# A fixed TensorE order and attention in five pieces, in a decoder layer of short convolution and retention

## The chip, the cores and the metric

The kernel runs on one core of one Trainium2 chip. The metric is the device time of one execution in microseconds; the time of a kernel is the median of its runs. Five engines matter: TensorE (PE in the profile; PEld is its weight load), VectorE (DVE), ScalarE (ACT), GpSimd (POOL) and SyncE (SP), which issues all the DMAs here. Each engine works through its own list of instructions in the order in which the list stands, and waits on semaphores for the others.

## The reference

One layer on 2048 rows of 1024 features with 16 learned meta rows ahead of them. The projection has eight parts of 512 columns: four for a gated convolution of width 3, four (q, k, v and a gate) for retention with four heads of 128. Retention is computed in chunks of 128 rows, with a state that is carried from chunk to chunk:

```python
hn = rms_norm(h, norm_g)
cx, cb, cc, cg, q, k, v, rg = jnp.split(hn @ w_in, N_PROJ, axis=-1)
conv_out = short_conv_branch(cx, cb, cc, conv_w) * silu(cg)
qf, kf = rotary(q) * RET_HEAD_DIM ** -0.5, rotary(k)
# per head and chunk of 128 rows
scores = (qc @ kc.T) * decay
inner = scores @ vc
upd = (kc * zeta).T @ vc
state = chunk_decay * state + upd            # cross uses the state before this chunk
cross = (qc * xi) @ state
ret = head_group_norm(inner + cross) * silu(rg)
out = rms_norm(h + concatenate([conv_out, ret]) @ w_out, final_g)
```

## The kernel before

Each float32 operand of a big product is split into a high and a low part (`wh`/`wl` for weights, `mh`/`ml` for the moving side), and three matmuls of 128x128 by 128x512 make one step; four steps, 12 matmuls, make one *product*. A *quad* computes a 2x2 block of results with seven such products (a Strassen-Winograd scheme, `quad`, matmul at L212). A *plain quad* (`quad_plain`, matmul at L262) does it with eight and needs no block sums; the first group, the first head of the second half and the first pair of output rows begin with plain quads. TensorE is fed from two rings of four PSUM banks: `pj` for the big products, `ms` for everything else.

The rows are handled in two halves (r = 0, 1). In each half the kernel goes through eight units: four convolution groups and four retention heads, in the order 4, 0, 1, 2, 3, 5, 6, 7 for r = 0 (4 is the first convolution group) and 0 to 7 for r = 1. Each unit has two quads: for a head first k and v, then q and the gate. After the second quad the head's attention follows in the source: for each half block j transposes of k and v (L631, L636), the state updates (L646), then for each j the scores (L659), the values (L669, L670), the norm on VectorE and GpSimd (L675 to L686), a transpose back (L693) and the gate with ret_norm_g (L694). The tile framework's scheduler decides at build time where each instruction stands on its engine; in before it mixes the pieces of a head's attention into the next unit's quads, and also orders single matmuls of the plain quads by when it expects their operands.

The start matters for the change. `moving` loads sixteen x tiles, scales them by norm1_g and splits them (L104, L105), with the first weight blocks in between (`begin`). After the eighth tile `normalise_meta` (L373 to L388) squares the meta tokens (L376), sums them on TensorE (L380), takes the root on VectorE and GpSimd (L275, L278), spreads it over the partitions (L285, L292, L295) and makes `meta_s` (L387, L388). `meta_products` (L390) multiplies `meta_s` with a unit's four raw weight blocks in 16 small matmuls (L397, two records each in the trace); its results feed the first state of each head and the first carry of each convolution group. For the first unit it is called, in the source, after `moving` and ahead of the first plain quad. While all this runs, `block_sums` (L174) and the splits of the second weights are queued on VectorE too.

Of the kernel before, what the change touches and what calls it, by code (L numbers as in the profile page):

```python
# [12 lines left out]
ALU = mybir.AluOpType  # L13

P = 128
D = 1024
SEQ = 2048
NMETA = 16
# [4 lines left out]
NR = 2  # L23
# [9 lines left out]
FIRST_W, PLAIN_W, B12 = 2, 3, 4  # L33
SUMS = (3, 2, 4, 6)

UNITS = (4, 0, 1, 2, 3, 5, 6, 7), (0, 1, 2, 3, 4, 5, 6, 7)
# [34 lines left out]
def hybrid_trunk(ctx: ExitStack, tc: tile.TileContext, t, out: bass.AP, chunk_decay):  # L71
# [14 lines left out]
    def ps_proj():  # L86
        return ps.tile([P, HB], F32, name="pj", tag="pj", bufs=4)

    def ps_misc():
# [113 lines left out]
    def quad(w, m, take):  # L203


        def product(i, bank, first):
            (wh, wl) = w[i]
            for kt in range(KH):
                ks = slice(kt * P, (kt + 1) * P)
                mh, ml = m[i][kt]  # L210
                for n, (a, b) in enumerate(((wl, mh), (wh, ml), (wh, mh))):
                    nc.tensor.matmul(  # L212
                        bank, a[:, ks], b, start=first and kt == 0 and n == 0, stop=kt == KH - 1 and n == 2,
                        skip_group_check=not first,
                    )

        def copy(bank):
            c = sb.tile([P, HB], F32, name="tc", tag="tc", bufs=COPIES)
            nc.scalar.copy(out=c, in_=bank)  # L219
            return c  # L220

        xb = ps_proj()
        product(0, xb, True)
        c = copy(xb)
        yb = ps_proj()
        product(1, yb, True)
        take(0, 0, yb, c)
        product(2, xb, False)
        u2 = copy(xb)
        zb = ps_proj()  # L230
        product(3, zb, True)
        c = copy(zb)
        product(4, xb, False)
        take(1, 1, xb, c)
        product(5, zb, False)
        take(0, 1, zb, u2)
        product(6, xb, False)
        take(1, 0, xb, None)

    def plain_part(n, load, slot):  # L240
# [10 lines left out]
    def quad_plain(w, m, take, middle=None):  # L251

        for j in range(2):
            banks = [ps_proj() for _ in range(2)]
            for half in range(2):
                for kt in range(KH):
                    ks = slice(kt * P, (kt + 1) * P)
                    mh, ml = m[BLOCK[half][j]][kt]
                    for i in range(2):
                        wh, wl = w[2 * i + half]  # L260
                        for n, (a, b) in enumerate(((wl, mh), (wh, ml), (wh, mh))):
                            nc.tensor.matmul(  # L262
                                banks[i], a[:, ks], b, start=half + kt + n == 0,
                                stop=half == 1 and kt == KH - 1 and n == 2,
                            )
            for i in range(2):
                take(i, j, banks[i], None)
            if middle and j == 0:
                middle()
# [120 lines left out]
    def meta_products(blocks, early=False):  # L390

        bank = ps_misc()
        four = [bank[i * 32 : i * 32 + NMETA, :P] for i in range(4)]
        with tc.high_priority(offset=HIGH) if early else nullcontext():
            for kt in range(KH):
                for i in (3, 2, 1, 0):
                    nc.tensor.matmul(  # L397
                        four[i], meta_s[:, i % 2 * KH + kt, :], blocks[i][:, kt * P : (kt + 1) * P],
                        start=kt == 0, stop=kt == KH - 1,
                    )  # L400
# [11 lines left out]
    def meta_state(h, scratch):  # L412
# [9 lines left out]
        add(nc.vector, k, a, b)  # L422
        up = ps_misc()
        nc.tensor.matmul(up[:, :P], k, v, start=True, stop=True)
        nc.scalar.copy(out=state[h], in_=up[:, :P])

    def meta_carry(g, scratch):

        cc, cx, u, _ = meta_sums(scratch)
        nc.vector.tensor_tensor(out=u, in0=cc, in1=cx, op=ALU.mult)  # L430
        tp = ps_misc()
        nc.tensor.transpose(tp[:, :NMETA], u, ident[:NMETA, :NMETA])
        nc.vector.tensor_copy(out=conv_carry[g], in_=tp[:, NMETA - 2 : NMETA])

# [29 lines left out]
    def group_plain(g, m, f, meta, first, between, ahead):  # L464
# [16 lines left out]
        quad_plain(first[0], m, take)  # L481
        meta_carry(g, meta)

# [31 lines left out]
    def conv_group(g, r, m, f, blocks, ahead):  # L515
# [20 lines left out]

        blocks, meta = blocks
        quad(stationary(blocks), m, take)
        if meta:
            meta_carry(g, meta)  # L540
        carry(u, g, r)
# [33 lines left out]
    def head(h, r, m, rot_t, f, blocks, ahead, first=(), between=()):  # L575


        between = iter(between)
        k, v = [None, None], [None, None]
        tables = [rot_t[:, :, j * HB : (j + 1) * HB] for j in range(2)]  # L580
# [17 lines left out]
        next(between, lambda: None)()  # L598
        q, sg = [None, None], [None, None]

# [21 lines left out]
        next(between, lambda: None)()  # L622
        if blocks[1]:
            meta_state(h, blocks[1])
        blocks = ahead()
        states = [state[h]]
        vt = []
        for j in range(2):
            tp = ps_misc()
            for c in range(CH):  # L630
                nc.tensor.transpose(tp[:, c * P : (c + 1) * P], k[j][:, c * P : (c + 1) * P], ident)  # L631
            kd = brief("kd")
            nc.scalar.mul(kd, tp, kd_col[:, h : h + 1])
            tp = ps_misc()
            for c in range(CH):
                nc.tensor.transpose(tp[:, c * P : (c + 1) * P], v[j][:, c * P : (c + 1) * P], ident)  # L636
            vj = v[j]
            for c in range(CH):
                cs = slice(c * P, (c + 1) * P)
                nc.scalar.mul(vj[:, cs], tp[:, cs], f[2][j][0][:, c : c + 1])  # L640
            vt.append(vj)
            last = r == NR - 1 and j == 1
            up = ps_misc()
            for c in range(CH - last):
                cs = slice(c * P, (c + 1) * P)
                nc.tensor.matmul(up[:, cs], kd[:, cs], vj[:, cs], start=True, stop=True)  # L646
            for c in range(CH - last):
                nxt = sb.tile([P, P], F32, name="state", tag="state", bufs=2 * CH)
                nc.vector.scalar_tensor_tensor(
                    out=nxt, in0=states[-1], scalar=chunk_decay[h], in1=up[:, c * P : (c + 1) * P],  # L650
                    op0=ALU.mult, op1=ALU.add,
                )
                states.append(nxt)

        for j in range(2):
            sc = ps_misc()
            for c in range(CH):
                cs = slice(c * P, (c + 1) * P)
                nc.tensor.matmul(sc[:, cs], k[j][:, cs], q[j][:, cs], start=True, stop=True)  # L659
            pm = brief("pm")  # L660
            nc.vector.scalar_tensor_tensor(
                out=pm.rearrange("p (c i) -> p c i", c=CH), in0=sc.rearrange("p (c i) -> p c i", c=CH),
                scalar=past_col[:, h : h + 1],
                in1=causal.rearrange("p (c i) -> p c i", c=1).broadcast_to([P, CH, P]), op0=ALU.mult, op1=ALU.mult,
            )
            o = ps_misc()
            for c in range(CH):
                cs = slice(c * P, (c + 1) * P)
                nc.tensor.matmul(o[:, cs], pm[:, cs], vt[j][:, cs], start=True, stop=False)  # L669
                nc.tensor.matmul(o[:, cs], q[j][:, cs], states[j * CH + c], start=False, stop=True)  # L670

            st = small.tile([P, CH, 6], F32, name="st", tag="st")
            mv = small.tile([P, CH, 2], F32, name="mv", tag="mv")
            for c in range(CH):
                nc.vector.bn_stats(out=st[:, c, :], in_=o[:, c * P : (c + 1) * P])  # L675
            for c in range(CH):
# [5 lines left out]
            nc.gpsimd.tensor_tensor(out=rp, in0=rs, in1=neg_half.rearrange("p (c a) -> p c a", a=1), op=ALU.pow)  # L682
            y = pm
            for c in range(CH):
                cs = slice(c * P, (c + 1) * P)
                nc.vector.tensor_scalar(  # L686
                    out=y[:, cs], in0=o[:, cs], scalar1=mv[:, c, 0:1], scalar2=rp[:, c, :],
                    op0=ALU.subtract, op1=ALU.mult,
                )
            yT = ps_misc()  # L690
            for c in range(CH):
                cs = slice(c * P, (c + 1) * P)
                nc.tensor.transpose(yT[:, cs], y[:, cs], ident)  # L693
            nc.vector.scalar_tensor_tensor(  # L694
                out=sg[j], in0=yT, scalar=ret_g[:, h : h + 1], in1=sg[j], op0=ALU.mult, op1=ALU.mult
            )
            store_mixed(r, j, KH + h, sg[j])
        if r < NR - 1:
            nc.gpsimd.tensor_copy(out=state[h], in_=states[-1])
        return blocks  # L700

# [202 lines left out]
```

## Time and profile before

| what | value |
|---|---|
| time, median of 3 runs | 895.5 us (894.32 to 895.67) |
| the profiled execution's own time | 893.76 us |
| its span, first to last instruction | 892.0 us |
| mean granted TensorE clock | 0.999 |
| matmuls at L212 and L262 | 3024 and 384 |

Rows of the timeline and of the chain begin with the start and the duration in us, then engine, line, operation, `out<-in`, shape and count; in brackets stands how long the engine was idle before and what ended that. Rows of the windows view begin with the stretch and its length; then come the busy time and the count of PE, PEld, DVE, ACT and POOL in it (fewer engines where the view was asked for one line, tile or engine), the granted clock, the DMA share and GB/s. Durations of neighbouring instructions overlap a little, so the spacing of starts is what one costs.

### The profile page before, as it was taken

To read this page: it belongs to the slowest core of one execution; us is meant where nothing else is said; L and a number is where in the kernel's file an instruction comes from. 1 tells how busy PE (TensorE), PEld (TensorE's weight loads), DVE (VectorE), ACT (ScalarE), POOL (GpSimd) and SP (SyncE) were. 2 spreads that over 40 slices of the span, in tenths; PEclk is the share of its full clock that TensorE was granted. 3 is DMA by queue.
4 is the path that set the end of the run, shared out by engine and by line. 5 is a ranking of instruction groups with operands and counts; after the bars stand their busy time and mean duration, and the time that the engine had idled before them with its cause. 6 is when DMAs were issued, how large, how long until landed. Compare 5 with 4: busy or idle time off the path is not lost.

```text
span 892.0 us, 12867 instructions
## 1 busy us (share of the span) xinstructions
PE 879.8 (99%) x4407; PEld 725.0 (81%) x4407; DVE 717.7 (80%) x1176; ACT 407.2 (46%) x816; POOL 397.8 (45%) x291
## 2 busy tenths in 40 slices
PE   8999999999999999999999999999999999999996
PEld 5778788888888778888888888888888888788885
DVE  6788887988967966999889899777668699766764
ACT  8674424234245364746243332423333476545553
POOL 0554222313134654452323323345546454787773
PEclk9999999999999999999999999999999999999999
DMA  9711224354224252834135272313131393555532
GB/s 336 231 65 48 72 54 150 129 159 149 73 83 142 83 154 75 293 117 141 48 95 200 71 245 87 96 58 95 49 93 49 117 390 101 183 165 160 183 121 81
DMA packets 76242, 116.94 MB, mean 131 GB/s; under 512 B 7632, under 2 KB 24336, under 8 KB 76176
## 3 DMA queue, kind: packets, MB, share of 16 engines
q1 hardware_dynamic: 76176, 116.11, 40.3%
q8 instruction: 35, 0.57, 0.3%
q14 instruction: 31, 0.25, 0.1%
HBM read 90.92 MB, written 25.17 MB: 130 GB/s over the span
## 4 chain that ended last, share of the span: by engine, by line
PE 82%; DVE 8%; DMA 4%; issue 2%; ACT 2%; POOL 2%; SPq 0%; POOLq 0%; DVEq 0%; ACTq 0%
PE pj L212 66%; PE pj L262 6%; DVE ml L113 2%; PE ms L669 1%; PE ms L670 1%; PE ms L659 1%; PE ms L646 1%; DMA w<-in_w_out 1%; DMA ra<-in_w_in 1%; PE ms L397 1%; DVE wl L113 1%; PE ms L693 1%; DVE ml L105 1%; PE ms L631 1%; PE ms L636 1%
## 5 line engine op out<-in xcount | busy, mean ns | idle before, releaser
L212 PE MATMUL pj<-mh,wl 128*128 128x512 f32 x1008 | 399.1, 396 | 1.5 <-ACT wh L101 0.6
L212 PE MATMUL pj<-ml,wh 128*128 128x512 f32 x1008 | 393.3, 390 | 0.0
L212 PE MATMUL pj<-mh,wh 128*128 128x512 f32 x1008 | 393.0, 390 | 0.0
L101 ACT CAST wh<-ra 128x512 fp32r<-128x512 f32 x216 | 134.0, 621 | 311.0 <-PE pj L212 264.9
L212 PEld LDWEIGHTS pj<-mh,wl 128*128 128x128 f32 x1008 | 189.4, 188 | 43.2 <-issue 2.2
L113 DVE TENSOR_TENSOR wl<-ra,wh 128x512 fp32r<-128x512 f32 x216 | 194.1, 899 | 34.5 <-ACT wh L101 34.0
L212 PEld LDWEIGHTS pj<-mh,wh 128*128 128x128 f32 x1008 | 189.2, 188 | 39.9
L212 PEld LDWEIGHTS pj<-ml,wh 128*128 128x128 f32 x1008 | 189.5, 188 | 37.8 <-issue 0.5
L113 POOL TENSOR_TENSOR ra<-ra 128x512 f32<-128x512 f32 x72 | 112.8, 1566 | 84.1 <-DVE qg L614 32.3
L110 POOL TENSOR_TENSOR sa<-ra 128x512 f32<-128x512 f32 x36 | 54.9, 1526 | 120.6 <-DVE wl L113 53.1
L113 POOL TENSOR_TENSOR ra<-sa,ra 128x512 f32<-128x512 f32 x36 | 52.0, 1444 | 92.6 <-DVE wl L113 89.1
L219 ACT COPY tc<-pj 128x512 f32<-128x512 f32 x108 | 62.7, 580 | 0.0
L262 PE MATMUL pj<-ml,mh 128*128 128x512 f32 x128 | 50.2, 392 | 0.1
L262 PE MATMUL pj<-mh,mh 128*128 128x512 f32 x128 | 49.9, 392 | 0.0
L262 PE MATMUL pj<-mh,ml 128*128 128x512 f32 x128 | 48.7, 397 | 0.7 <-DVE ml L113 0.6
L682 POOL TENSOR_TENSOR rp<-rs,neg_half 128x4 f32<-128x4 f32 x16 | 19.9, 1246 | 48.1 <-DVE rs L110 47.8
L723 DVE TENSOR_TENSOR yo<-pj,yo 128x512 f32<-128x512 f32 x32 | 21.9, 686 | 17.6 <-PE pj L212 7.8
L101 ACT CAST wh<-sa 128x512 fp32r<-128x512 f32 x36 | 22.4, 621 | 29.1 <-PE pj L212 28.9
L522 POOL TENSOR_TENSOR c<-c,rr 128x512 f32<-128x512 f32 x14 | 26.1, 1865 | 19.6 <-DVE c L459 9.6
L686 DVE TENSOR_SCALAR pm<-ms,mv,rp 128x128 f32<-128x128 f32 x64 | 21.9, 404 | 15.8 <-POOL rp L682 15.8
L522 POOL TENSOR_TENSOR c<-c,tc 128x512 f32<-128x512 f32 x14 | 26.1, 1862 | 18.7 <-ACT tc L548 18.7
L728 POOL TENSOR_TENSOR z<-yo,final_g 128x512 f32<-128x512 f32 x16 | 26.9, 1682 | 15.9 <-DVE yo L723 15.9
(137 smaller groups left out, 1145.5 us busy)
## 6 DMA issues: line engine op xcount, KB each, us to landing
ra<-in_w_in SPq DMA_DIRECT2D x128, 256.0 KB, 2.7
x<-in_xT SPq DMA_DIRECT2D x48, 256.0 KB, 4.8
w<-in_w_out SPq DMA_DIRECT2D x32, 256.0 KB, 5.2
ra<-mixed SPq DMA_DIRECT2D x32, 256.0 KB, 2.6
yo<-in_x SPq DMA_DIRECT2D x32, 256.0 KB, 4.5
ra<-in_x SPq DMA_DIRECT2D x16, 256.0 KB, 3.2
mixed<-c SPq DMA_DIRECT2D x16, 256.0 KB, 2.6
mixed<-qg SPq DMA_DIRECT2D x16, 256.0 KB, 2.3
```

Of the source, the lines that this page charges most:

```text
L101: nc.scalar.copy(out=hi, in_=src)
L105: nc.vector.scalar_tensor_tensor(out=lo, in0=src, scalar=scale, in1=hi.bitcast(F32), op0=ALU.mult, op1=ALU.subtract)
L110: eng.tensor_tensor(out=out, in0=a, in1=b, op=ALU.add)
L113: eng.tensor_tensor(out=out, in0=a, in1=b, op=ALU.subtract)
L212: nc.tensor.matmul(bank, a[:, ks], b, start=first and kt == 0 and n == 0, stop=kt == KH - 1 and n == 2, skip_group_check=not first,)
L219: nc.scalar.copy(out=c, in_=bank)
L262: nc.tensor.matmul(banks[i], a[:, ks], b, start=half + kt + n == 0, stop=half == 1 and kt == KH - 1 and n == 2,)
L522: eng.tensor_tensor(out=out, in0=a, in1=b, op=ALU.mult)
L682: nc.gpsimd.tensor_tensor(out=rp, in0=rs, in1=neg_half.rearrange("p (c a) -> p c a", a=1), op=ALU.pow)
L686: nc.vector.tensor_scalar(out=y[:, cs], in0=o[:, cs], scalar1=mv[:, c, 0:1], scalar2=rp[:, c, :], op0=ALU.subtract, op1=ALU.mult,)
L723: last[0] = nc.vector.tensor_tensor(out=y, in0=pp, in1=y, op=ALU.add)
L728: nc.gpsimd.tensor_tensor(out=ys[i][j], in0=y, in1=final_g[:, j * HB : (j + 1) * HB], op=ALU.mult)
```

## The change

Two things are changed. First, every big matmul, every attention matmul and transpose, and the meta products (all but the ones marked early) go through `pinned`, which ties each to the one before it in the source: the scheduler can no longer reorder these on TensorE. The warm-up, the small matmuls in `normalise_meta` and those in `spread` stay free.

Second, the attention of a head becomes five pieces. They are handed out at the head's start and called behind products that the table PLACES gives as (quads from here, product): for a head that is not the first (1, 1), (1, 6), (2, 1), (2, 4), (3, 1). So the first piece (transposes of block 0) comes in the head's second quad behind product 1; the second (transposes of block 1, meta state, updates of block 0) behind its last product; the third (updates of block 1, both scores) in the next unit's first quad behind product 1; the fourth (both values, with the norm) behind product 4; the last (both gates) in the next unit's second quad behind product 1, where the next head's first piece also stands. The meta state and the meta carry put their TensorE part into a function that is called at such a place.

```diff
+PLACES = ((1, 3), (1, 6), (2, 2), (2, 4), (3, 1)), ((1, 1), (1, 6), (2, 1), (2, 4), (3, 1))
...
+    def pinned(ins):
+        if last_pe:
+            tc.add_manual_dep(
+                ins.ins, last_pe.pop(),
+                mybir.DependencyInfo(mybir.DependencyClass.NoSync, mybir.DependencyReason.DATA), reason="order",
+            )
+        last_pe.append(ins.ins.name)
+    def matmul(*a, **k):
+        pinned(nc.tensor.matmul(*a, **k))
+    def transpose(*a):
+        pinned(nc.tensor.transpose(*a))
+    def at(quads, p, piece):
+        due.setdefault((count[0] + quads, p), []).append(piece)
+    def after_product(p):
+        for piece in due.pop((count[0], p), ()):
+            piece()
+        if p == 6:
+            count[0] += 1
...
         product(1, yb, True)
         take(0, 0, yb, c)
+        after_product(1)
...
+                if half == 0:
+                    after_product(3 * j)
+                    after_product(3 * j + 1)
             for i in range(2):
                 take(i, j, banks[i], None)
+            for p in (5, 6) if j else (2,):
+                after_product(p)
...
+        mm = nc.tensor.matmul if early else matmul
         with tc.high_priority(offset=HIGH) if early else nullcontext():
             for kt in range(KH):
                 for i in (3, 2, 1, 0):
-                    nc.tensor.matmul(
+                    mm(
...
+        for place, piece in zip(PLACES[h > 0], attention(h, r, f, k, v, q, sg, blocks[1])):
+            at(*place, piece)
...
+        def first():
+            if meta:
+                finish[0] = meta_state(h, meta)
+            turn(0)
+        def second():
+            turn(1)
+            finish[0]()
+            update(0)
+        def third():
+            update(1)
+            scores(0)
+            scores(1)
+        def fourth():
+            values(0)
+            values(1)
+            if r < NR - 1:
+                nc.gpsimd.tensor_copy(out=state[h], in_=states[-1])
+        def last():
+            gate(0)
+            gate(1)
+        return first, second, third, fourth, last
```

Three places in the order, row by row. The first is TensorE at the start, behind the warm-up. Before, the first rows and, in the second fence, the place of the first meta products further on (`meta_s`; `ra` are raw weight blocks, `pj` the products' banks, mh/ml the split operands):

```order
L262 MATMUL pj<-mh_115,ml_122 128x512
L262 MATMUL pj<-ml_116,mh_121 128x512
L262 MATMUL pj<-mh_115,mh_121 128x512
L262 MATMUL pj<-mh_115,ml_128 128x512
L262 MATMUL pj<-ml_116,mh_127 128x512
L262 MATMUL pj<-mh_115,mh_127 128x512
```

```order
L262 MATMUL pj<-mh_145,ml_281 128x512
L262 MATMUL pj<-ml_146,mh_280 128x512
L397 MATMUL ms<-ra,meta_s 16x128 x16
L262 MATMUL pj<-mh_145,mh_280 128x512
L262 MATMUL pj<-mh_145,ml_287 128x512
```

Now, right behind the warm-up (L423 are the sums of normalise_meta, L335 its spread, L104 every pinned matmul):

```order
L423 MATMUL ms<-ones,state_83 16x1 x8
L335 MATMUL ms<-rot,ones 128x16
L104 MATMUL ms<-ra,meta_s 16x128 x16
L104 MATMUL pj<-mh_115,ml_122 128x512
L104 MATMUL pj<-ml_116,mh_121 128x512
L104 MATMUL pj<-mh_115,mh_121 128x512
```

The meta products have moved from behind the 116th product to the head of the list, and the sums and the spread that they need stand ahead of them.

The second place is VectorE at the start, between the last splits of x and `meta_s` (`state_82` holds the meta tokens, `rm` their factors, `t` and `x` block sums). Before, the rows that end with it:

```order
L113 TENSOR_TENSOR ml_293<-ra,mh_292 128x512
L113 TENSOR_TENSOR ml_299<-ra,mh_298 128x512
L174 SCALAR_TENSOR_TENSOR x<-x,gain 128x512
L113 TENSOR_TENSOR ml_316<-x,mh_315 128x512
L174 SCALAR_TENSOR_TENSOR x<-x,gain 128x512
L387 TENSOR_TENSOR state_82<-state_82,rm 128x128
L113 TENSOR_TENSOR ml_320<-x,mh_319 128x512
L388 TENSOR_TENSOR meta_s<-state_82,gain 128x128
```

Now, from the last split of x on; ahead of these rows stand, behind the second t step (t_307), rs_v, five splits of x, the diagonal `rot` and three more splits:

```order
L136 SCALAR_TENSOR_TENSOR ml_253<-x,gain,mh_252 128x512
L144 TENSOR_TENSOR ml_281<-ra,mh_280 128x512
L205 SCALAR_TENSOR_TENSOR x<-x,gain,t_306 128x512
L144 TENSOR_TENSOR ml_287<-ra,mh_286 128x512
L430 TENSOR_TENSOR state_82<-state_82,rm 128x128
L205 SCALAR_TENSOR_TENSOR x<-x,gain,t_307 128x512
L144 TENSOR_TENSOR ml_293<-ra,mh_292 128x512
L144 TENSOR_TENSOR ml_299<-ra,mh_298 128x512
L205 SCALAR_TENSOR_TENSOR x<-x,gain 128x512
L431 TENSOR_TENSOR meta_s<-state_82,gain 128x128
```

`meta_s` has moved ahead by three rows of 512 columns and by an eviction of the first product that stood further up; the rest of the queue ahead of it is the same.

The third place is VectorE between a head's values and its gates (`st`, `mv`, `rs`, `rp`: the norm's statistics; `pm` its result; `kv` and `rot`: the next unit's k). Before, for block 0 of the first head; block 1's statistics follow eighteen rows further on:

```order
L675 BN_STATS st<-ms 128x6 x4
L677 BN_AGGR mv<-st 128x2 x4
L110 TENSOR_TENSOR rs<-mv,ev 128x4
L686 TENSOR_SCALAR pm<-ms,mv,rp 128x128 x4
L110 TENSOR_TENSOR kv<-pj,tc 128x512
L113 TENSOR_TENSOR wl<-ra,wh 128x512
L570 TENSOR_TENSOR rot<-kv,rot_t 64x512
```

Now, for both blocks; four statistics, four aggregations and the sum rs of block 0 stand just ahead:

```order
L724 BN_STATS st<-ms 128x6 x4
L726 BN_AGGR mv<-st 128x2 x3
L733 TENSOR_SCALAR pm<-ms,mv,rp 128x128 x4
L726 BN_AGGR mv<-st 128x2
L141 TENSOR_TENSOR rs<-mv,ev 128x4
L141 TENSOR_TENSOR kv<-pj,tc 128x512
L144 TENSOR_TENSOR wl<-ra,wh 128x512
L622 TENSOR_TENSOR rot<-kv,rot_t 64x512
L623 TENSOR_TENSOR rot<-kv,rot_t 64x512
L733 TENSOR_SCALAR pm<-ms,mv,rp 128x128 x4
```

Both blocks' norms now stand together, with one take, one split and two rotation steps between them.

119 lines of the change are left out of this document (58 added, 61 removed).

## The prediction

> **What bounds the kernel now.** I read the busy line of the page first, then the windows view for one quarter of the run and for what is left, then the timeline of the first 37 us, and last the places where TensorE stood.
>
> ```profile
> PE 879.8 (99%) x4407; PEld 725.0 (81%) x4407; DVE 717.7 (80%) x1176; ACT 407.2 (46%) x816; POOL 397.8 (45%) x291
> 36.41:885.30 848.89, 846.36 (x4236) 1.00 0.39 124
> 36.41:885.30 848.89, 707.16 (x3024) 562.50 (x3024) 1.00 0.39 124
> 36.41:885.30 848.89, 63.17 (x268) 50.00 (x268) 1.00 0.39 124
> 36.41:885.30 848.89, 102.97 (x944) 1.00 0.39 124
> 767.63 117.31 PE pj L212 x516
> 155.30 0.89 PE ms L646 x8
> ```
>
> TensorE is the bound: 99% busy, 846.4 of 848.9 us in the long stretch. That busy time hides small gaps, because a matmul's end overlaps the next one's start, so I count work instead. The sixth row, from the chain, gives 117.31 / 516 = 0.227 us for a 512-column product; the seventh 0.89 / 8 = 0.111 us for a 128-column one. Between 36.41 and 885.30 stand 3024 + 268 of the first kind (L212, L262) and 944 on the misc banks, of which seven groups of 32 are packed meta products that take 1.0 us a group (a row below). 3292 x 0.2273 + 720 x 0.111 + 7 = 748 + 80 + 7 = 835 us. So of 848.9 us at most 14 can be waits: that is all that a better order could win there.
>
> **The start, which the change rewrites.** The timeline of before, by engine:
>
> ```profile
> 2.29 3.63 PE L766 MATMUL ms<-warm 128*128 128x512 bf16 x9 [2.29 <-ACT warm L760]
> 6.12 0.50 PE L262 MATMUL pj<-mh,ml 128*128 128x512 f32 x1 [0.20 <-DVE ml L113]
> 13.35 0.28 DVE L376 TENSOR_TENSOR state<-state 128x128 f32<-128x128 f32 x1
> 15.08 0.55 PE L380 MATMUL ms<-ones,state 128*16 128x1 f32 x16
> 16.20 1.41 DVE L105 SCALAR_TENSOR_TENSOR ml<-x,gain,mh 128x512 fp32r<-128x512 f32 x2
> 17.53 0.14 DVE L275 TENSOR_SCALAR rs_v<-ms 16x1 f32<-16x1 f32 x1
> 17.60 3.38 DVE L105 SCALAR_TENSOR_TENSOR ml<-x,gain,mh 128x512 fp32r<-128x512 f32 x5
> 17.82 0.92 POOL L278 TENSOR_TENSOR rc<-rs_v,neg_half 16x1 f32<-16x1 f32 x1 [16.48 <-DVE rs_v L275]
> 20.91 0.16 DVE L285 TENSOR_TENSOR rot<-ident,rc 16x16 f32<-16x16 f32 x1
> 20.99 1.40 DVE L105 SCALAR_TENSOR_TENSOR ml<-x,gain,mh 128x512 fp32r<-128x512 f32 x2
> 23.58 1.27 DVE L113 TENSOR_TENSOR ml<-ra,mh 128x512 fp32r<-128x512 f32 x2
> 24.78 0.73 DVE L174 SCALAR_TENSOR_TENSOR x<-x,gain,t 128x512 f32<-128x512 f32 x1
> 29.19 1.37 DVE L113 TENSOR_TENSOR ml<-x,mh 128x512 fp32r<-128x512 f32 x1 [0.34 <-ACT mh L101]
> 30.49 1.38 DVE L388 TENSOR_TENSOR meta_s<-state,gain 128x128 f32<-128x128 f32 x1
> 35.41 1.07 PE L397 MATMUL ms<-ra,meta_s 128*16 128x128 f32 x32
> 36.41 0.50 PE L262 MATMUL pj<-mh,mh 128*128 128x512 f32 x1
> ```
>
> Before, the first product starts at 6.12, as soon as one x tile and one weight block are split. The normalised meta tokens (meta_s) come off VectorE at 30.49 + 1.38 = 31.9, and the meta products run at 35.41. Ahead of them stand 384 - 268 = 116 of the L262 products: 26.4 us of work at 0.227.
>
> **Part 1: the meta products stand first.** meta_products is called ahead of the first quad in the source, and its matmuls are now links of TensorE's chain. In the new order all 116 products stand behind it, so nothing of them starts before meta_s is there. When is that? I follow VectorE's new order in the change section. Up to t_307 it is that of before, done at 16.20. Then: rs_v 0.07; five splits of 0.66 each (17.60 to 20.91 holds five): 19.6; the diagonal `rot`, whose input from GpSimd was ready by then, 0.08; four splits of 0.66: 22.3; then ml_281, ml_287, ml_293 and ml_299 at 0.60 (23.58 to 24.78 holds two), three `x` steps of the kind at 24.78, taken at 0.66, and the 128x128 step 0.2, together 4.6: 26.9. meta_s itself took 1.38: **28.3**. Its small matmuls find TensorE idle and cost nothing on this path, and the copy of the factors on ScalarE has from the diagonal (19.7) until the 128x128 step (24.2) to get through.
>
> The meta products take 1.0 us (35.41 to 36.41): 29.3. Then TensorE is in the state that before had at 36.41, less 116 products. 29.3 + 26.4 - 36.4 = **+19.3 us**. Before spent 29.3 us, from 6.12 to 35.41, on these 26.4 us of work, so hardly anything was waiting there to be won back.
>
> **Part 2: the cold clock.**
>
> ```profile
> 885.30:889.00 3.70, 0.00 (x0) 0.00 (x0) 2.08 (x5) 1.72 (x4) 0.55 (x1) 1.00 0.38 142
> 889.00:892.00 3.00, 0.00 (x0) 0.00 (x0) 0.00 (x0) 0.00 (x0) 0.00 (x0) 0.57 0.46 175
> ```
>
> The nine warm-up matmuls took 3.63 us, 0.40 each, for the columns that later take 0.227; after the last product the granted clock fell to a mean of 0.57 some 4 us on (second row). In the new start TensorE has next to nothing to do from 5.9 to 28, so I take the clock as fallen and pay once more what the nine cost above full speed: 3.63 - 9 x 0.227 = **+1.6 us**. Bounds: nothing, if the small matmuls hold the clock, and twice that, 3.2. [...]
>
> **Part 3: the attention pieces.** Instruction for instruction they are what they were, and a change between 512 and 128 columns costs nothing that the timeline shows. So the work does not change; only waits can. Most pieces now have more room: the scores come before the values by two or three products of 12 x 0.227 = 2.7 us. The tightest is values to gate: four products, 10.9 us.
>
> ```profile
> 169.63 0.88 DVE L675 BATCH_NORM_STATS2 st<-ms 128x6 f32<-128x128 f32 x4
> 170.43 0.36 DVE L677 BATCH_NORM_AGGREGATE mv<-st 128x2 f32<-128x6 f32 x4
> 172.30 1.37 DVE L686 TENSOR_SCALAR pm<-ms,mv,rp 128x128 f32<-128x128 f32 x4 [1.13 <-POOL rp L682]
> 173.58 0.68 DVE L110 TENSOR_TENSOR kv<-pj,tc 128x512 f32<-128x512 f32 x1
> 174.89 0.69 DVE L570 TENSOR_TENSOR rot<-kv,rot_t 64x512 f32<-64x512 f32 x1
> 155.30:205.68 50.38, 50.38 (x292) 42.10 (x292) 44.11 (x91) 18.87 (x40) 14.71 (x11) 1.00 0.41 137
> ```
>
> In that time VectorE has, by its new order, two statistics of 0.8, two aggregations of 0.4, two scalings of 1.28 (172.30 to 173.58), an add and a split of 0.6, two rotations of 0.7 and one wait for GpSimd of 1.1: 8.7 us of 10.9. It fits with 2 us to spare, in an engine that is busy 44 of 50 us. Term: **0**, bounds -1 and +1 us for each of eight heads.
>
> **Part 4: the waits of before, and the seams.**
>
> ```profile
> 62.12 0.39 PE L212 MATMUL pj<-mh,wh 128*128 128x512 f32 x1
> 63.01 0.50 PE L212 MATMUL pj<-mh,wl 128*128 128x512 f32 x1 [0.51 <-ACT tc L219]
> 509.34 0.39 PE L212 MATMUL pj<-mh,wh 128*128 128x512 f32 x1
> 510.01 0.33 PE L693 MATMUL ms<-ident,pm 128*128 128x128 f32 x1 [0.28 <-DVE pm L686]
> 510.18 0.60 PE L631 MATMUL ms<-ident,kv 128*128 128x128 f32 x4
> ```
>
> The later start gives the other engines a lead at the first Strassen quad, so the 0.66 us at 62.12 goes, and the gate of 509.34 (0.44) stands later now: with the smaller ones **-1.5**. Against it, twice (second half of the rows, then output) the scheduler had put 17 plain products ahead of the last quad's end; the source order takes that back. What was late there is data, and the strict turn of the two banks asks for it up to five products, 1.1 us, sooner: two seams, taken at **+1.5**, bounds 0 and 2.3. SP's order and its loads at the start are the same.
>
> **Sum.** 893.8 (the profiled run's own time) + 19.3 + 1.6 + 0 - 1.5 + 1.5 = 914.7. The median of the runs shown, 895.5, lies 1.7 above the profiled run; I add some of that and say **916**.
>
> **The rivals.** *The pieces wait.* If VectorE misses its 2 us of room, the gate piece holds up the products behind it by what it lacks; an estimated 1 us in each of eight heads makes 923. For it: VectorE's load. Against: the counted 8.7 of 10.9.
>
> *The lead pays.* VectorE and GpSimd run ahead while TensorE stands, and half of the 14 us of possible waits goes: 908. Against: most of their work hangs on TensorE's own banks, so a lead cannot be stored for long.
>
> *The order does not hold.* If TensorE passed over a matmul that waits, the first products would start at 6 as before, and only won waits would be left: with half of the 14 us, 887, faster. It decides from the point at which the products may run ahead of meta_s. Against it stands 509.34: TensorE stood still for pm while the transposes of 510.18, of another head and with their data there, waited behind it. [...]
>
> *The meta chain runs bare.* After 13.63 its rows alone need 0.55 + 0.14 + 0.92 + 0.16 + 1.38 = 3.2 us; without any queue meta_s stands at 16.8 and the start costs 16.8 + 1.0 + 26.4 - 36.4 = 7.8, which more than half of the 14 us of waits would have to pay: 894, no change. The new order has 19 long VectorE steps between, so this needs another order than the printed one.
>
> **How the numbers follow.** Forecast, 912 to 920: 0.62. Pieces wait, 920 to 927: 0.18. Lead pays, 904 to 912: 0.16. Order does not hold: 0.02, faster. Bare chain: 0.02, within 0.2%, which is about what a measurement of this kernel can tell from no change. The start alone moves by -1.1 (meta_s in 0.28, as the 128x128 step at 13.35, where it took 1.38) and by +2 (splits that double like the one at 29.19), the clock by 1.6 either way. The range 908 to 925 leaves out the ends of the second and third case and the last two. Faster 0.02, same 0.02, slower 0.96.
>
> **What would show it.** In the timeline after: the first plain product at 29 to 31 instead of 6.12, behind meta products at 28 to 29; products 0.43 apart for some 3 us; then heads of 50.4 us as before, and no TensorE wait over 1 us at a gate. I would be wrong if plain products run before 25, if meta_s stands much later than 28, or if the heads' period leaves 50 to 51 us.

## The result, and the profile after

| | us |
|---|---|
| the changed kernel, median of 6 runs | 915.9 (914.49 to 916.88) |
| before, median of 6 runs on the same chip | 894.9 (894.32 to 895.67) |
| ratio | 1.0232, 95% interval 1.0219 to 1.0245 |
| the profiled execution of the changed kernel, its span | 914.49, 912.7 |

The change costs 21 us. The page of the changed kernel, its busy line and TensorE's row of the 40 slices:

```profile
PE 878.0 (96%) x4407; PEld 728.3 (80%) x4407; DVE 714.7 (78%) x1176; ACT 408.6 (45%) x816; POOL 402.6 (44%) x291
PE   2899999999999999999999999999999999999996
```

TensorE does the same 4407 matmuls in nearly the same busy time (879.8 before). What is new is a hole: the first slice of 22.8 us is 2 tenths busy, and from the third on TensorE is as full as before. The timeline of the start shows what the hole waits for:

```profile
13.58 0.56 PE L423 MATMUL ms<-ones,state 128*16 128x1 f32 x16 [7.27 <-DVE state L419]
19.59 0.60 PE L335 MATMUL ms<-rot,ones 16*128 16x16 f32 x2 [5.45 <-DVE rot L328]
26.71 0.27 DVE L431 TENSOR_TENSOR meta_s<-state,gain 128x128 f32<-128x128 f32 x1
27.04 1.91 PE L104 MATMUL ms<-ra,meta_s 128*16 128x128 f32 x32 [6.85 <-DVE meta_s L431]
28.88 0.80 PE L104 MATMUL pj<-mh,ml 128*128 128x512 f32 x1
31.18 0.63 PE L104 MATMUL pj<-mh,mh 128*128 128x512 f32 x1
31.60 0.47 PE L104 MATMUL pj<-mh,ml 128*128 128x512 f32 x1
31.92 0.39 PE L104 MATMUL pj<-ml,mh 128*128 128x512 f32 x1
32.15 0.39 PE L104 MATMUL pj<-mh,mh 128*128 128x512 f32 x1
```

Three waits of 7.3, 5.5 and 6.9 us, one for each step of the meta chain, and then the first plain product at 28.88 instead of 6.12. Up to 31.60 the products stand 0.42 apart (31.18 to 31.60), from 31.92 on 0.23. The rest of the run shows in the waits view (for whom TensorE waited: us in total, times, longest). The changed kernel, without the start:

```profile
PE pj L104 <- DVE wl L144: 2.1, 1, 2.1
PE pj L104 <- DVE tc L141: 1.6, 1, 1.6
PE pj L104 <- DVE ml L144: 1.2, 1, 1.2
PE pj L104 <- ACT tc L250: 0.4, 1, 0.4
```

The same view of before:

```profile
PE pj L212 <- ACT wh L101: 0.6, 1, 0.6
PE pj L262 <- DVE ml L113: 0.6, 2, 0.4
PE pj L212 <- ACT tc L219: 0.5, 1, 0.5
PE ms L693 <- DVE pm L686: 0.3, 1, 0.3
```

Before, no wait is longer than 0.6 us. After, three are longer than 1 us, none of them at an attention piece: one for the weights of a quad (`wl`, behind the first head), and two at the seams to the second half of the rows (`tc`) and to the output (`ml`).

To see where in the run the time is lost, I count the 512-column matmuls of the `pj` banks through both traces (3408 records in each) and compare the start of the n-th:

| n-th product | before, us | after, later by | what lies ahead of it |
|---|---|---|---|
| first | 6.12 | 22.8 | |
| 250 | 70.63 | 19.8 | the start |
| 1600 | 439.88 | 20.1 | the heads of the first half, the first seam |
| 2700 | 722.95 | 19.8 | the second half |
| last | 884.54 | 20.7 | the second seam, the output |

Nearly all of the loss is there at product 250. It is smaller than at the first product because before did the meta products and some waiting in between. The rows stand where both kernels have about as many small matmuls behind them (87 each at 250, 990 each at 2700, 700 and 692 at 1600); elsewhere the difference swings, from 23.6 us at product 600 to 16.1 at 1200, since the pieces of attention stand at other places among the products.

### The profile page after: what moved, and what is told of

It reads as the page before. It is cut to its first block, busy times and chain, and to the rows that moved or that the text cites. A ratio compares the mean times of both kernels' runs of the same rounds, so it can differ in the third digit from the quotient of the medians.

```text
span 912.7 us, 12892 instructions
## 1 busy us (share of the span) xinstructions
PE 878.0 (96%) x4407; PEld 728.3 (80%) x4407; DVE 714.7 (78%) x1176; ACT 408.6 (45%) x816; POOL 402.6 (44%) x291
## 4 chain that ended last, share of the span: by engine, by line
PE 85%; DVE 6%; DMA 4%; ACT 3%; issue 2%; POOL 1%; SPq 0%; POOLq 0%; DVEq 0%; ACTq 0%
PE pj L104 75%; PE ms L104 7%; PE ms L107 2%; ACT mh L135 1%; DMA w<-in_w_out 1%; DVE wl L144 1%; DVE ml L144 1%; DMA ra<-mixed 1%; ACT mh L132 1%; DMA t<-sums_w 1%; DVE ml L136 1%; PE ms L335 0%; DVE c L524 0%; DMA ra<-in_w_in 0%; ACT wh L132 0%
## 5 line engine op out<-in xcount | busy, mean ns | idle before, releaser
L104 PE MATMUL pj<-mh,wl 128*128 128x512 f32 x1008 | 397.6, 394 | 4.3 <-DVE wl L144 2.1
L104 PE MATMUL pj<-ml,wh 128*128 128x512 f32 x1008 | 392.6, 389 | 0.0
L104 PE MATMUL pj<-mh,wh 128*128 128x512 f32 x1008 | 392.5, 389 | 0.0
L104 PEld LDWEIGHTS pj<-mh,wl 128*128 128x128 f32 x1008 | 189.3, 188 | 47.6 <-issue 4.4
L144 DVE TENSOR_TENSOR wl<-ra,wh 128x512 fp32r<-128x512 f32 x216 | 184.1, 855 | 47.1 <-ACT wh L132 46.7
L104 PEld LDWEIGHTS pj<-mh,wh 128*128 128x128 f32 x1008 | 189.2, 188 | 39.7
L104 PEld LDWEIGHTS pj<-ml,wh 128*128 128x128 f32 x1008 | 189.4, 188 | 38.0 <-ACT mk L447 0.2
L144 POOL TENSOR_TENSOR ra<-ra 128x512 f32<-128x512 f32 x72 | 120.6, 1676 | 85.1 <-DVE state L700 48.5
L141 POOL TENSOR_TENSOR sa<-ra 128x512 f32<-128x512 f32 x36 | 52.9, 1469 | 121.8 <-DMA ra<-in_w_in 41.7
L104 PE MATMUL pj<-mh,ml 128*128 128x512 f32 x128 | 51.2, 400 | 1.2 <-DVE ml L144 1.2
L104 PE MATMUL pj<-mh,mh 128*128 128x512 f32 x128 | 50.7, 396 | 0.0
L104 PE MATMUL pj<-ml,mh 128*128 128x512 f32 x128 | 50.3, 393 | 0.0
L141 DVE TENSOR_TENSOR tc<-pj,tc 128x512 f32<-128x512 f32 x28 | 19.3, 688 | 19.2 <-PE pj L104 19.0
L797 ACT ACTIVATE rot<-yo 128x512 f32<-128x512 f32 x32 | 20.2, 630 | 29.9 <-DVE yo L795 29.5
```

The costliest lines, as they stand in the source:

```text
L104: pinned(nc.tensor.matmul(*a, **k))
L141: eng.tensor_tensor(out=out, in0=a, in1=b, op=ALU.add)
L144: eng.tensor_tensor(out=out, in0=a, in1=b, op=ALU.subtract)
L797: nc.scalar.activation(junk, y, AF.Square, accum_out=ss[:, i, j : j + 1])
```

## The experiments

Theory 1: the start is the loss, a hold of about 19 us and a clock that has to come up again, and the fixed order costs nothing after it. Theory 2, the rival: the start would be made up for by the lead of the other engines, and the fixed order costs a little at each of its many places. The first four kernels tell these apart.

**The hold taken away (e1).** In the changed kernel the first unit's meta products are taken out of the chain (`free=True` has `meta_products` call `nc.tensor.matmul` without `pinned`); all else stays pinned.

```diff
-            blocks = None, meta_products([a for a, p in w])
+            blocks = None, meta_products([a for a, p in w], free=True)
```

> The changed kernel with one call altered: the first unit's meta products are not links of TensorE's chain, so the scheduler may put them where it likes; all else is tied as before, and the five pieces stay. Theory 1 (the loss is the start alone: 20.2 us of hold and cold clock by the trace, and the rest of the change nets to nothing): 895, within 2 us of the kernel before, the first plain product near 6 us. Theory 2 (the fixed order costs waits all along, and the start is partly won back later): 903 to 912.

Measured: 897.3 us (895.33 to 898.12), ratio to before 1.0030 (1.0016 to 1.0044). The first product starts at 6.35. One call of 16 matmuls, let go, gives back 17.9 of 21 us (each kernel set against before on its own chip). What is left, 3.1 us over before, is more than the 2 us that theory 1 allowed. It belongs to the fixed order and its pieces; in the profiled execution 1.6 us of the loss are a stretch at a granted clock of 0.52 that the last section shows.

**The hold alone (e2).** In the kernel before, the first plain quad's matmuls are tied behind the meta products; nothing else is fixed.

```diff
+                            if len(hold) == 1:
+                                tc.add_manual_dep(
+                                    ins.ins, hold[0],
...
+        if not hold and not early:
+            hold.append(mine.ins.name)
```

> The kernel before, with one thing added: the first plain quad's matmuls may not stand ahead of the meta products. Nothing else is tied and attention is as before. Theory 1: 915, within 2 us of the changed kernel, with its first plain product near 29 us and 0.427 us apart for some 3 us. Theory 2: clearly less, 900 to 910, since free matmuls elsewhere win part of it back.

Measured: 913.9 us (913.57 to 914.29), ratio 1.0220 (1.0205 to 1.0235). Its timeline starts like that of the changed kernel:

```profile
27.11 1.91 PE L407 MATMUL ms<-ra,meta_s 128*16 128x128 f32 x32 [6.84 <-DVE meta_s L396]
28.94 0.80 PE L262 MATMUL pj<-mh,ml 128*128 128x512 f32 x1
```

By the count of products it is 20.0 us behind before at product 250, and 20.0 at the last: one hole, and not a tenth won or lost in the 814 us that follow. That excludes *the lead pays* for the order of before, too.

**Also the plain quads free (e3).** e1, with the matmuls of `quad_plain` out of the chain.

```diff
-                            matmul(
+                            nc.tensor.matmul(
                                 banks[i], a[:, ks], b, start=half + kt + n == 0,
```

> As e1_meta_free, and the matmuls of the plain quads are free too; the Strassen products and attention stay tied. The changed kernel waits 1.8 us at 397.5 and 1.3 us at 754.4, where a tied quad meets a plain one. Theory 1a (these waits come of the plain quads' place in the chain): 2 to 3 us under e1_meta_free, some 892. Rival (VectorE's splits are late there in any order): within 1 us of e1_meta_free.

Measured: 894.5 us (892.95 to 896.58), ratio 1.0005 (0.9994 to 1.0016). The seam waits of e1, 1.6 (`tc`) and 1.2 us (`ml`), fall to under 0.2 and to 0.7. So the strict order of the plain quads, where the scheduler of before set single matmuls by their operands, costs 2.8 us by the medians of e1 and e3, and 1.7 between their two profiled executions. One wait for `wl`, 2.2 us at 106.56, is still there.

**The pieces, nothing pinned (e5).** The source of the changed kernel with the chain taken away altogether.

```diff
-        pinned(nc.tensor.matmul(*a, **k))
+        nc.tensor.matmul(*a, **k)
...
-        pinned(nc.tensor.transpose(*a))
+        nc.tensor.transpose(*a)
```

> The changed kernel with its five pieces in their places in the source, and nothing tied: the scheduler orders all of TensorE. Theory 1: 895, within 2 us of before, since the pieces alone neither add work nor waits. Rival (the pieces cost waits at the gates by themselves): 900 or more.

Measured: 895.8 us (894.2 to 896.87), ratio 1.0018 (1.0008 to 1.0027). Cutting the attention into five pieces wins nothing by itself; it costs 1.5 us, and its interval lies just above 1.

**The clock kept up (e4).** The changed kernel, with the sums and the spread of the meta tokens in the chain and 24 matmuls of zeros behind them, so that TensorE works until the meta products begin.

```diff
+        wp = ps_misc()
+        for _ in range(24):
+            matmul(
+                wp.rearrange("p (a c) -> p a c", a=CH), warm,
+                warm.rearrange("p (a c) -> p a c", a=1).broadcast_to([P, CH, P]), start=True, stop=True,
+            )
```

> The changed kernel, with 24 matmuls of bf16 zeros (128x512) put behind the spread of the meta factors, all in the fixed order, so that TensorE works until the meta products begin; nothing else is changed. Theory 'the start costs an idle stretch plus a cold clock': the meta products and the first plain products run at full speed (pitch 0.227 us from the first plain product instead of 0.427), the start of the meta products stays within 0.5 us of 27.0, and the time falls by 1.5 to 2.2 us against the changed kernel, to 913.7 to 914.4 us. Rival 'the half speed at the start costs nothing, since those products wait for their operands (the arrival of x) anyway': the pitch becomes 0.227 but with gaps, and the time stays within 0.5 us of 915.9. If the spread is late because the sums now stand in the fixed order, the meta products begin later than 27.5 and the time rises by as much.

Measured: 915.9 us (915.03 to 916.87), ratio 1.0238 (1.0222 to 1.0253): nothing won. The timeline of e4, first the start, then the place where the gain goes:

```profile
20.19 6.73 PE L104 MATMUL ms<-warm 128*128 128x512 bf16 x24
27.14 1.07 PE L104 MATMUL ms<-ra,meta_s 128*16 128x128 f32 x32 [0.23 <-PE ms L104]
28.14 0.50 PE L104 MATMUL pj<-mh,ml 128*128 128x512 f32 x1
...
38.15 1.03 POOL L321 TENSOR_TENSOR rc<-rs_v,neg_half 128x4 f32<-128x4 f32 x1
39.38 0.39 PE L104 MATMUL pj<-ml,mh 128*128 128x512 f32 x1
39.95 0.68 DVE L328 TENSOR_TENSOR rot<-ident,rc 128x512 f32<-128x512 f32 x1
40.69 0.70 PE L335 MATMUL ms<-rot,ones 128*128 128x512 f32 x1 [0.92 <-DVE rot L328]
```

The step that was meant did happen: the meta products take 1.0 us (1.84 from start to start in the changed kernel), the products stand 0.23 apart from 28.48 on, and by the 20th product e4 is 2.1 us ahead of the changed kernel. But at 39.38 the row factors' spread (L335) stands in TensorE's list and waits for VectorE's `rot`, which comes no earlier for TensorE's lead (39.95 here, 39.53 in the changed kernel). TensorE then stands 1.1 us more, and 0.7 more at the second spread at 46.7; the changed kernel waits 0.4 in all there. At product 250 only 0.6 us of the 2.1 are left, and two waits further on (1.6 at 113 and 1.2 at 351, where the changed kernel has none and 0.6) eat more than that. Theory's mechanism holds, its price does not: the rival, that these products would wait anyway, gives the right time.

**The wait behind the first head (e7, e9, e10, e11).** What holds `wl`? In the changed kernel's timeline:

```profile
119.33 1.07 PE L104 MATMUL ms<-ra,meta_s 128*16 128x128 f32 x32
120.53 1.70 POOL L144 TENSOR_TENSOR ra<-ra 128x512 f32<-128x512 f32 x1 [13.49 <-DVE qg L625]
120.39 4.08 DVE L524 TENSOR_TENSOR c<-c,cb 128x512 f32<-128x512 f32 x3
124.59 1.58 DVE L524 TENSOR_TENSOR c<-c,cb 128x512 f32<-128x512 f32 x1
126.50 0.91 DVE L700 SCALAR_TENSOR_TENSOR state<-state,ms 128x128 f32<-128x128 f32 x3
127.33 0.68 DVE L144 TENSOR_TENSOR wl<-ra,wh 128x512 fp32r<-128x512 f32 x1
128.16 0.47 PE L104 MATMUL pj<-mh,wl 128*128 128x512 f32 x1 [2.10 <-DVE wl L144]
```

Two readings offer themselves. GpSimd may be late: it overwrites the raw weights `ra` in place, so it waits until the next unit's meta products have read them (119.33 + 1.07 = 120.40), and these stand behind the first head's second piece in the fixed order. Or VectorE is late: `c`, `mk` and the states stand ahead of `wl` in its list, without a gap. I took the first for the cause. e7 (from e3) and e9 (from the changed kernel) move the second piece behind product 0 of the next quad, so that the meta products come ahead of its transposes and updates.

```diff
-PLACES = ((1, 3), (1, 6), (2, 2), (2, 4), (3, 1)), ((1, 1), (1, 6), (2, 1), (2, 4), (3, 1))
+PLACES = ((1, 3), (2, 0), (2, 2), (2, 4), (3, 1)), ((1, 1), (1, 6), (2, 1), (2, 4), (3, 1))
```

> The kernel e3_meta_and_plain_free (894.5 us; first meta products and plain quads out of the fixed order) with one entry of the table of places changed: the first head's second piece comes behind product 0 of the next quad ((2, 0) for (1, 6)), so the next unit's meta products stand ahead of it in TensorE's order, 20 matmuls earlier. Theory 'the first head's wait of 2.3 us comes from the order: GpSimd may overwrite the raw weights of the next quad only when the meta products have read them, and the pieces hold these back': the meta products run at 97.7 instead of 100.2, GpSimd's difference of weights begins at 98.9 instead of 101.4, the wait at 106.56 falls from 2.3 to under 0.3, and the time falls by 1.9 to 2.4 us to 892.1 to 892.6, which is 1.6 to 2.1 us less than the kernel before. Rival 'the wait comes from VectorE, which does 4 products c<-c,cb and the rotary work ahead of the split wl': the wait stays over 1.5 us and the time within 0.7 us of 894.5.

> The changed kernel with the first head's second piece behind product 0 of the next quad, (2, 0) for (1, 6), and nothing else. If the wait of 2.27 us at 125.7 in the changed kernel comes from this one place, it falls under 0.6 and the time is 913.3 to 914.2 us. If the wait is made by VectorE's queue instead, or if what is won there is lost at the seams behind it, the time stays at 915.2 or above.

Measured: e7 892.3 us (890.27 to 893.18), ratio 0.9972 (0.9962 to 0.9983), where e3 had 894.5; e9 913.9 us (912.99 to 914.7), ratio 1.0222 (1.0208 to 1.0236), where the changed kernel had 915.9. The timeline of e9 at that place:

```profile
116.94 1.07 PE L104 MATMUL ms<-ra,meta_s 128*16 128x128 f32 x32
118.14 1.48 POOL L144 TENSOR_TENSOR ra<-ra 128x512 f32<-128x512 f32 x1 [11.09 <-PE ms L104]
125.67 0.67 DVE L144 TENSOR_TENSOR wl<-ra,wh 128x512 fp32r<-128x512 f32 x1
126.49 0.47 PE L104 MATMUL pj<-mh,wl 128*128 128x512 f32 x1 [0.41 <-DVE wl L144]
```

Times and rows fall where the theory put them: meta products and GpSimd 2.4 us earlier, the wait down from 2.1 to 0.4. The gain of e9 is small, though: against before on its own chip it is 19.9 us slower, where the changed kernel is 21.0, and the two intervals overlap. Nor does this settle the cause, for the edit also took the states from ahead of `wl` to behind it on VectorE. e10 and e11 leave TensorE's list word for word as it was, in the changed kernel and in e7, and only put the four `c` later.

```diff
-        next(between, lambda: None)()
+        at(0, 3, next(between, lambda: None))
         return ahead()
```

> The changed kernel with the last four products of the first convolution group on VectorE (c<-c,cb) put later in the source, behind product 3 of the next unit's first quad; TensorE's list is word for word that of the changed kernel, so the next unit's meta products stay behind the second piece (119.3) and GpSimd's differences stay at 120.5. What e9 moved were the meta products, but with them four state updates left their place ahead of the split wl on VectorE, so e9 can't tell two causes apart. Theory 'GpSimd is late, because the meta products are late': the wait of 2.1 to 2.3 us for wl at 125.7 stays over 1.5 us and the time at 915.3 to 916.5. Rival 'VectorE is late, since it has c, mk and the states ahead of wl without a gap from 118.5 to 127.3': the high part wh is ready at 124.6 in the changed kernel, wl follows at once and stands at 125.3, ahead of the 125.9 at which TensorE asks for it; the wait falls under 0.4 us and the time to 913.4 to 914.4.

> e7_meta_ahead_of_second (892.3 us) with the same four products of VectorE later; TensorE's list is that of e7. If VectorE is what is late behind the first head, the rest of the wait there (0.6 us at 105.5) goes and the time is 891.5 to 892.1; if GpSimd is, the wait and the time of 892.3 stay within 0.3 us. Should the four products now hold up the scores' pm or a later split, a wait shows between 108 and 125 us and the time rises.

Measured: e10 912.7 us (911.96 to 913.32), ratio 1.0206 (1.0192 to 1.0220); e11 891.3 us (890.2 to 891.86), ratio 0.9966 (0.9952 to 0.9979). The timeline of e10, and its row of the waits view for `wl`:

```profile
119.92 1.07 PE L104 MATMUL ms<-ra,meta_s 128*16 128x128 f32 x32
121.12 1.30 POOL L144 TENSOR_TENSOR ra<-ra 128x512 f32<-128x512 f32 x1 [13.49 <-DVE qg L625]
124.47 1.23 DVE L144 TENSOR_TENSOR wl<-ra,wh 128x512 fp32r<-128x512 f32 x1 [0.35 <-ACT wh L132]
PE pj L104 <- DVE wl L144: 0.2, 1, 0.2
```

GpSimd is as late as ever (120.53 in the changed kernel, 121.12 here, with a start that is 0.6 later), and the wait is gone. The time fell a little further than the 913.4 to 914.4 expected. So VectorE was late, not GpSimd, and my theory of e7 and e9 falls although its numbers came out. Why is VectorE late? The view of the tile `c` has the four products (shortest, median and longest in ns, first and last start), first in the changed kernel:

```profile
L524 DVE TENSOR_TENSOR c<-c,cb x4: 684/1680/1778, 120.4 to 124.6; 128x512 f32<-128x512 f32 x4
```

and in e10:

```profile
L524 DVE TENSOR_TENSOR c<-c,cb x4: 676/678/679, 133.5 to 136.8; 128x512 f32<-128x512 f32 x4
```

Beside GpSimd's three differences (120.5 to 125.6) such a product takes up to 1.78 us. In e10, behind the differences, each takes 0.68, and so does a VectorE step of the same shape at 119.07 in the changed kernel, where GpSimd stands idle (13.49 us, up to 120.53). It also fits with what the earlier meta products of e9 did: GpSimd was through sooner (123.0 for 125.6), and three of its four `c` were short again (median 676 ns in the same view). So, as far as these rows show, GpSimd matters after all, but by when its differences run beside VectorE's `c` and not by its own lateness. Why a product takes longer there was not tested.

e11 has the lowest time of this study, 3.0 us less than before, but its interval overlaps that of e7, so these runs don't tell the two apart. By the starts of the products e7's wait of 0.57 us at 105.5 is gone, as expected of a late VectorE; two waits further on, at 288 and 328, have grown from 0.37 to 0.97 each.

**Many small interruptions (e8).** e7 waits no less than before and is still faster. I summed TensorE's time from the first head on, from the starts of the matmuls: the distance of two neighbouring products above 0.227 us is waiting; where small matmuls stand between two products, that distance and the next one count as an interruption, above two pitches.

| from the first head on | waits between products, us | interruptions | their sum, us |
|---|---|---|---|
| before | 2.8 | 67 | 94.2 |
| e2 | 2.8 | 67 | 94.3 |
| changed | 8.0 | 38 | 89.9 |
| e5, pieces not pinned | 4.2 | 76 | 94.7 |
| e7 | 4.0 | 39 | 89.9 |
| e8, pieces split | 7.8 | 71 | 90.8 |

The fixed order does the same small matmuls in 38 interruptions instead of 67, for 4.3 us less, or 0.15 us each. e8 tests whether it is the number: e7 with nine pieces a head instead of five.

```diff
+REST = ((2, 1), (2, 2), (2, 3), (2, 4), (2, 5), (3, 1), (3, 2))
+PLACES = ((1, 3), (2, 0)) + REST, ((1, 1), (1, 6)) + REST
...
+        return first, second, third, fourth, lambda: scores(1), sixth, seventh, lambda: gate(0), lambda: gate(1)
```

> The kernel e7_meta_ahead_of_second (892.3 us) with its five attention pieces per head cut into nine, which stand behind products of their own; the operations and their order among themselves stay. So each of eight heads interrupts the products four times more, 32 in all, for the same small matmuls. Theory 'each interruption of the 512-column products costs by itself': in the traces so far the interruptions from the first head on took, above the pitch of the products, 94.2 us in 67 of them (before) and 89.9 us in 38 (changed) for the same small matmuls, which is 0.15 us each; so 32 more cost 4.7 us, the interruptions take about 94.5 us, and the time is 896 to 898 us. Rival 'the interruptions cost nothing and the difference of the sums comes from waits inside of them': the sum stays within 1 us of e7's 89.9 us and the time within 1 us of 892.3, or it moves by what the lists of waits show.

Measured: 894.7 us (893.95 to 896.07), ratio to before 1.0005 (0.9996 to 1.0014). The theory falls: with 71 interruptions the sum is 90.8, so one costs (90.8 - 89.9) / 32 = 0.03 us and not 0.15. The 2.4 us that e8 is slower than e7 go with its waits (7.8 against 4.0). So the 4.3 us are inside the interruptions. Of before's 94.2, 1.9 us are four waits at the edge of an interruption: 0.70 at 305.3, 0.46 at 106.1, 0.44 at 509.3 (for `pm`) and 0.31 at 92.9; the changed kernel has none over 0.1. Of the other 2.4 us about 1.9 lie at the meta products. Before breaks the 32 records of a unit up into two or three interruptions, and together these take about 1.5 to 1.8 us above the pitch in five units of six, once the other small matmuls there are taken off at what they cost elsewhere; in one go, as in the changed kernel and in e8, they take 1.2 (e8 at 97.30). e8 left them whole, so it did not test this; e5, where they are broken up again, is back at 94.7 us. Why the broken ones cost more is open.

## Why the prediction was right, point by point

The forecast was 916 us and the time 915.9. Its steps came out unequally well.

- **Part 1, the hold, was right in its mechanism and 1 us too large.** e2 does this one thing and costs 20.0 us by the count of products, 19.7 by the medians. The prediction gave 19.3 + 1.6 = 20.9. `meta_s` was put at 28.3 and stood at 27.0: the step took 0.27 us and not 1.38, the bound that the text had named. VectorE's order up to it was followed to 0.2 us. With 27.0 for 28.3 the hold is 18.0, and with the 2.1 us of the next point the sum is 20.1, which is what e2 costs.
- **Part 2, the cold clock, happened as described (products 0.42 apart up to 31.60), but 1.6 us is not what it costs.** The first cost is even larger, 2.1 us at the 20th product, since the meta products are slow as well (1.84 us where e4 has 1.00), which the term had left out. Yet most of that is hidden: the second wait, for the row factors, stands right behind it. At product 250 e4 was 0.6 us better, and at its end not at all. The step that failed is that TensorE's loss at the start would all arrive at the end; I had not looked at what TensorE waits for next. The products leave the spacing of 0.42 at 31.60 in the changed kernel, 4.6 us after the meta products begin, and at 30.80 in e2, 3.7 us after.
- **Part 3, the pieces, was right at 0 only as a sum.** No gate was waited for by over 1 us, and the window of one head, 170.01 to 220.15, is 50.14 us where 50.4 were expected. That a change between 512 and 128 columns costs next to nothing is shown by e8 (0.03 us). What was missed is a gain: the fixed order does the interruptions in 4.3 us less.
- **Part 4, the waits, was too small on the losing side.** The two waits named, at 62.12 and 509.34, are gone. The seams cost 1.6 + 1.2 = 2.8 us by the waits view and by the medians of e1 and e3 (1.7 between their profiled executions), where 1.5 was taken and 2.3 was the upper bound. And a wait of 2.1 us that no step had foreseen stands behind the first head. The prediction asked at each gate whether the piece's data is there, but not what the piece adds to VectorE's list: here its states and a group's four `c`, up to 1.78 us long beside GpSimd's differences where e10 has 0.68, stood ahead of the split that the next quad needs (e10). Together the waits between products rise by 8.0 - 2.8 = 5.2 us, against the 4.3 won in the interruptions: +0.9, where the prediction had 0.
- **The rivals.** *The pieces wait* is out in the form it had: no wait stands at a piece, though the `c` and the states on VectorE did hold up a product behind the first head. *The lead pays* is out: e2 is 20.0 us behind at product 250 and at the last, and the changed kernel 19.8 and 20.7. *The order does not hold* and *the meta chain runs bare* are out by the start, with the first plain product at 28.88 and `meta_s` at 26.98.

So the right total rests on one large term, 20 us of 21, that was right to 1 us, and on two small ones of opposite sign, 4 and 5 us, that were not seen. That the hold and clock came out 0.9 too large and the rest 0.9 too small, so that 916 meets 915.9, is luck.

## What to carry to other kernels

When an order is fixed in the source, look first at its first link that waits: here one early call of 16 small matmuls cost 20 us (e2 was 20.0 us behind at product 250, and still at the last), while the rest of the change, its gains set against its waits, cost 1.3 us with that call (21.0 less 19.7) and 3.1 without it (e1). For every link that moves ahead, ask not only whether its data is there but what it puts ahead of whom on the other engines; taking one link out of the chain was worth 17.9 us, and moving four VectorE instructions behind a split that TensorE waits for took away 1.9 us of a wait of 2.1. A slow stretch that ends just ahead of a wait for another engine can cost less than its length (of the 2.1 us that e4 had won by the 20th product, 0.6 were left at product 250 and nothing at the end), so follow a term to the next wait before it goes into the sum.

## What the runs showed that was not expected

In the changed kernel the granted clock misses a slow stretch. The windows view of the changed kernel and of e4 (stretch and length; busy time and count of PE, PEld, DVE, ACT and POOL; granted clock; DMA share and GB/s), first the changed kernel:

```profile
13.00:20.00 7.00, 0.97 (x18) 0.92 (x18) 7.00 (x14) 7.00 (x13) 0.92 (x1) 1.00 1.05 408
27.00:32.00 5.00, 4.96 (x40) 3.70 (x41) 3.67 (x5) 4.29 (x13) 3.48 (x2) 1.00 0.85 255
```

Then e4:

```profile
13.00:20.00 7.00, 0.92 (x18) 0.86 (x18) 7.00 (x14) 7.00 (x13) 0.92 (x1) 0.50 1.06 405
20.00:27.00 7.00, 6.92 (x26) 2.75 (x25) 7.00 (x14) 2.28 (x7) 3.35 (x1) 0.78 0.57 195
```

Between 13 and 20 us both kernels do the same, and one record says 1.00, the other 0.50. In the changed kernel the row says 1.00 for 27 to 32 us while the products stand 0.42 apart. Its trace has no entry of the clock before 31.8 us, and the view puts 1.00 where it has none. There the distance of equal matmuls, 0.42 against the later 0.23, is the better clock.

In e1 a slow stretch follows a wait. The wait for `wl` behind the first head is followed by this (the last row is the windows view of TensorE alone):

```profile
108.87 0.68 PE L104 MATMUL pj<-mh,wl 128*128 128x512 f32 x1 [2.14 <-DVE wl L144]
109.35 0.63 PE L104 MATMUL pj<-ml,wh 128*128 128x512 f32 x1
109.78 0.63 PE L104 MATMUL pj<-mh,wh 128*128 128x512 f32 x1
...
112.60 0.39 PE L104 MATMUL pj<-mh,wl 128*128 128x512 f32 x1
112.83 0.39 PE L104 MATMUL pj<-ml,wh 128*128 128x512 f32 x1
108.80:112.20 3.40, 3.33 (x8) 0.52 0.47 98
```

For 3.4 us the products stand 0.43 apart, and the granted clock, 0.52, agrees here. With some 0.2 us for each of eight products, another 1.6 us are lost behind the wait of 2.14. In the changed kernel the products behind the same wait (2.10 at 128.16) stand 0.23 apart from 128.47 on. What decides between the two was not tested. So the remainder of e1 can hold this price beside the wait itself.
